# Four block sums per spilled block of a ConvFFN: from GpSimd to VectorE

## Chip, cores and metric

The kernel runs on one core of a Trainium2 chip. The metric is the device time of one execution in microseconds; 2660.22 us is the median of three runs before the change.

## What is computed

The kernel computes a two-layer diffusion trunk over 1024 tokens of 1024 channels. Layer 0 mixes by a long convolution beside differential attention, layer 1 by a chunked gating MLP, and each layer ends with a ConvFFN, the part that the change touches. Cut to that part, the reference is:

```python
D_MODEL, SEQ, D_FF = 1024, 1024, 2816

def dwconv3(u, w, b):
    up = jnp.pad(u, ((0, 0), (1, 1), (0, 0)))
    return up[:, :-2] * w[0] + up[:, 1:-1] * w[1] + up[:, 2:] * w[2] + b

def conv_ffn(h, w_up, conv_w, conv_b, w_down):
    a = dwconv3(h @ w_up, conv_w, conv_b)
    g, u = jnp.split(a, 2, axis=-1)
    return (jax.nn.silu(g) * u) @ w_down
...
for i in range(2):
    ...
    x = x + g1 * mix_x
    x = x + g2 * conv_ffn(modulate(rmsnorm(x, norm_ffn_g[i]), sh2, sc2), ffn_w_up[i], ...)
```

## The kernel before, in words

Every large matrix product of these phases is rewritten in two ways. First, each float32 operand is split into a high part in the fp32r format and a residual, and a product is three matmuls (high x high, high x low, low x high; `mm3`). Second, the operands are cut into 2x2 blocks and multiplied by a Strassen-Winograd scheme with seven products M1 to M7 instead of eight, which needs sums of blocks of each operand beforehand. The seven blocks of the activation side are called B11, B21, B22, T1, T2, T3, T4, and the last four are sums.

A ConvFFN has an up phase and a down phase, and the kernel runs the pair twice, once per layer: the first up phase lies at about 950 to 1420 us, the second at about 1950 to 2420 us. The hidden width 2816 is 22 blocks of 128 rows. An up phase goes through the blocks f = 0, 11, 1, 12, ..., 10, 21, so that two blocks that belong together (k and k + 11) follow each other. For each block f the seven products run in the order M1, M2, M5, M6, M4, M3, M7, with twelve matmuls of 128x128 by 128x512 each, which is 84 a block and 168 a pair; the first three blocks are interleaved. M6 accumulates onto the PSUM bank of M1, M7 onto that of M6, M3 onto that of M5 (`ONTO`, line 1299), so M1's bank must have been copied out before M6 may start. ScalarE does this copy at line 1331, and the others at lines 1337, 1339 and 1341; VectorE adds the rest (lines 1334, 1344, 1347).

The weights of a block are loaded by the SP queue (line 1308), summed by VectorE (`wsums`, line 1288) and split by `hilo_w` (line 1140). Where VectorE is not chosen for the residual, `hilo_w` makes the high part with ScalarE (line 1145), writes its negative with ScalarE (line 1146) and has GpSimd issue a DMA that accumulates the original onto it (line 1147). In the first up phase five of seven products go that way, in the second six of seven (`E_W`, line 56). `hilo` (line 1133) makes the residual with a subtraction on VectorE or GpSimd instead (line 1137).

After M7 of a block, `gated` (line 1589) runs as a background generator, advanced once per step of the main order (`Later.tick`): the convolution as one ScalarE operation (line 1583) and two VectorE operations (lines 1584 and 1586) for each of the two halves, the silu on ScalarE (line 1595), and the product of gate and value on VectorE (line 1597). After every second block it calls `spill` (line 1431), which computes the four sums T1 to T4 of the pair and writes seven blocks to a DRAM tensor Td with four stores. The stores are issued from ScalarE's queue (`st`, line 97). The four sums are the subject of this change. There are 11 spills in an up phase, 22 in all. All additions and subtractions go through the helper of line 132, so profile rows of line 132 hold many uses.

The down phase (`down_steps`, line 1365) reads the blocks back from Td by the SP queue, splits them with `hilo` on GpSimd (line 1472), prepares its weights with sums and residuals on VectorE and GpSimd, and accumulates into the residual stream.

The order of the instructions on each engine is fixed when the kernel is built: a scheduler walks the program in order of priority, where `tc.high_priority(PP)` moves weight preparation and the emptying of banks ahead. At run time each engine takes its instructions strictly in that order, and DMA issues stand in the same queue as the work of the engine that issues them. Tiles named `u` (40 buffers) hold nearly everything in these phases, and `b` is a PSUM bank.

Of the kernel before, what the change touches and what calls it, by code (L numbers as in the profile page):

```python
# [92 lines left out]
def tile_kernel(ctx: ExitStack, tc: tile.TileContext, ap: dict, out: bass.AP, stop=None):  # L93
    nc = tc.nc
    V, A, G, T = nc.vector, nc.scalar, nc.gpsimd, nc.tensor
# [34 lines left out]
    def binop(op):  # L130
        def f(eng, o, a, b):
            eng.tensor_tensor(out=o, in0=a, in1=b, op=op)  # L132
        return f

    add, sub, mul = binop(ADD), binop(SUB), binop(MUL)
# [120 lines left out]
    H0, H1 = slice(0, 512), slice(512, 1024)  # L256
# [870 lines left out]
    def unit(dt=F32):  # L1127
        return up.tile([P, S], dt, tag="u", name=nm("u"))
# [25 lines left out]
    class Later:  # L1154
# [3 lines left out]
        @classmethod  # L1158
        def add(cls, gen, wait=0):
            cls.gens.append([gen, wait])  # L1160
# [270 lines left out]
    def spill(Td, k, b1, b2):  # L1431

        t, s = unit(), unit()
        st(Td[0, :, k], b1[:, H0])
        st(Td[1:3, :, k].rearrange("a p n -> p a n"), b2.rearrange("p (a n) -> p a n", a=2))
        sub(G, s[:, H0], b2[:, H1], b1[:, H1])
        yield 1
        add(G, t[:, H1], s[:, H0], b1[:, H0])
        yield 1
        sub(G, s[:, H1], b2[:, H0], t[:, H1])  # L1440
        st(Td[5:7, :, k].rearrange("a p n -> p a n"), s.rearrange("p (a n) -> p a n", a=2))
        yield 1
        sub(G, t[:, H0], b1[:, H1], b1[:, H0])
        st(Td[3:5, :, k].rearrange("a p n -> p a n"), t.rearrange("p (a n) -> p a n", a=2))

    def in_place(s, m, k, y, z, t3, first="M6"):
# [129 lines left out]
    def ffn(l, after, dst):  # L1576
# [12 lines left out]
        def gated(f, c1, c2):  # L1589
            box = []  # L1590
            yield from conv(c2, NF + f, box)
            yield 1
            yield from conv(c1, f, box)
            u, g = box
            A.activation(g, g, AF.Silu)
            yield 1
            mul(V, g, g, u)
            acts[f] = g
            yield 1
            if f >= nk:  # L1600
                yield from spill(Td, f - nk, acts.pop(f - nk), acts.pop(f))
# [267 lines left out]
```

## Time and profile before

| | us |
|---|---|
| median of three runs | 2660.22 |
| lowest, highest | 2655.24, 2663.31 |
| the profiled execution: its own time | 2657.56 |
| the profiled execution: span from first to last instruction | 2655.8 |
| busy: TensorE matmul / weight load | 2461.9 / 1964.8 |
| busy: VectorE / ScalarE / GpSimd | 1811.5 / 1205.4 / 874.9 |
| granted TensorE clock, mean over the span | 0.972 |

The profile is of one execution. PE is TensorE (PEld its weight loads), DVE is VectorE, ACT is ScalarE, POOL is GpSimd, and a q behind a name is the engine's sequencer, which issues DMAs. A row of a group has line, engine, operation, output and inputs with tile names, the form and the count, then the busy time and the mean of one in ns, and then the idle time of the engine just before such instructions with what ended it. A row of a timeline starts with the start in us and the duration; in square brackets stands how long the engine was idle before it and who released it. "u<-u" alone means that all inputs come from one tile, "u<-u,u" that they come from two. A row of waits has who waited for whom, the total, the number of times and the longest. A granted clock of 1.00 is the full 2.4 GHz.

### The profile page before, as it was taken

How to read it: one execution, taken by the hardware profiler on the slowest of the kernel's cores; microseconds unless marked ns; L12 is line 12 of the kernel's file. 1: busy time of each engine (PE TensorE's matmuls, PEld its weight loads, DVE VectorE, ACT ScalarE, POOL GpSimd, SP SyncE). 2: the span in 40 equal slices, each digit the busy share in tenths (PEclk: the TensorE clock that was granted, in tenths of full speed). 3: DMA queues.
4: the chain of work that ended last, by engine and by line, in shares of the span. 5: the costliest groups of instructions: out<-in, count | busy, mean ns of one | idle time of the engine just before them, and what ended most of it. 6: DMA issues, size and time to landing. Idle time of an engine off the chain costs nothing. (4 is left out here: it accounts for less than half of the span.)

```text
span 2655.8 us, 30417 instructions
## 1 busy us (share of the span) xinstructions
PE 2461.9 (93%) x11192; PEld 1964.8 (74%) x11192; DVE 1811.5 (68%) x2297; ACT 1205.4 (45%) x1875; POOL 874.9 (33%) x649
## 2 busy tenths in 40 slices
PE   6889998798889999999999999999999999999897
PEld 1678987676767776777777787878877777777676
DVE  4888878979995666665656967543467555567844
ACT  2421121137674565655555354323466656564342
POOL 1200112304442013232326574000014343448674
PEclk9999999899999999999999999999999999999998
DMA  7123334277722657888878534012447777778422
GB/s 292 52 103 119 122 105 140 83 222 217 208 69 72 215 136 190 217 229 207 230 193 302 174 120 158 24 47 88 133 90 159 179 176 164 180 175 311 143 74 97
DMA packets 167270, 412.75 MB, mean 155 GB/s; under 512 B 16043, under 2 KB 29359, under 8 KB 164944
## 3 DMA queue, kind: packets, MB, share of 16 engines
q1 hardware_dynamic: 86768, 248.76, 29.3%
q0 software_dynamic: 34848, 63.45, 14.0%
q10 hardware_dynamic: 45504, 98.58, 10.0%
q8 instruction: 88, 1.44, 0.2%
q14 instruction: 62, 0.51, 0.1%
HBM read 261.31 MB, written 85.98 MB: 131 GB/s over the span
## 5 line engine op out<-in xcount | busy, mean ns | idle before, releaser
L154 PE MATMUL b<-u,u 128*128 128x512 f32 (+1 forms) x5624 | 1316.8, 393 | 46.0 <-POOL u L132 19.3
L154 PEld LDWEIGHTS b<-u,u 128*128 128x128 f32 x5624 | 1054.9, 190 | 307.1 <-POOL u L132 26.7
L132 DVE TENSOR_TENSOR u<-u,u 128x512 fp32r<-128x512 f32 (+2 forms) x525 | 470.3, 924 | 314.5 <-ACT u L1136 133.6
L132 POOL TENSOR_TENSOR u<-u,u 128x512 fp32r<-128x512 f32 (+1 forms) x283 | 432.7, 1552 | 189.2 <-ACT u L1136 102.9
L1147 POOL DMA_DIRECT2D u<-u x242 | 211.2, 918 | 560.7 <-ACT u L1146 421.5
L1136 ACT CAST u<-u 128x512 fp32r<-128x512 f32 x462 | 261.4, 616 | 226.7 <-DVE u L132 106.6
L154 PE MATMUL b<-x,u 128*128 128x512 f32 x1224 | 298.5, 399 | 2.7 <-DMA u<-u 2.7
L128 DVE SCALAR_TENSOR_TENSOR u<-u,cols,u 128x1023 f32<-128x1023 f32 x176 | 231.8, 1324 | 95.8 <-ACT u L1583 87.3
L154 PEld LDWEIGHTS b<-x,u 128*128 128x128 f32 x1224 | 230.5, 189 | 64.2 <-DMA u<-u 3.5
L132 POOL TENSOR_TENSOR wlo<-wraw,whi 128x1024 fp32r<-128x1024 f32 x24 | 79.7, 3327 | 401.3 <-ACT whi L147 401.3
L1145 ACT CAST u<-u 128x512 fp32r<-128x512 f32 x242 | 146.3, 615 | 105.5 <-DVE u L132 89.3
L1146 ACT ACTIVATE u<-u 128x512 fp32r<-128x512 f32 x242 | 149.3, 628 | 79.0 <-POOL u L132 70.2
L132 DVE TENSOR_TENSOR u<-u,b 128x512 f32<-128x512 f32 (+1 forms) x132 | 112.4, 861 | 76.6 <-PE b L154 71.1
L132 DVE TENSOR_TENSOR f<-f 128x256 f32<-128x256 f32 (+3 forms) x276 | 152.0, 614 | 0.5 <-DMA Hd<-f 0.2
L1583 ACT ACTIVATE u<-u,cols 128x1024 f32<-128x1024 f32 x88 | 109.2, 1241 | 81.8 <-DVE u L132 81.2
L154 PE MATMUL pj<-hh,whi 128*128 128x512 f32 x320 | 129.1, 405 | 15.6 <-ACT t L736 8.3
L154 PE MATMUL pj<-hl,whi 128*128 128x512 f32 x320 | 128.6, 402 | 3.4 <-DVE hl L132 3.4
L154 PE MATMUL pj<-hh,wlo 128*128 128x512 f32 x320 | 128.2, 401 | 0.0
L128 DVE SCALAR_TENSOR_TENSOR x<-b,mods,x 128x512 f32<-128x512 f32 (+1 forms) x104 | 88.8, 907 | 57.7 <-PE b L154 57.7
L132 POOL TENSOR_TENSOR p<-p,p 128x1280 f32<-128x1280 f32 x27 | 80.1, 2969 | 121.7 <-ACT p L880 103.7
L869 ACT ACTIVATE p<-s,nx 128x1280 f32<-128x1280 f32 x64 | 85.0, 1328 | 45.2 <-DVE nx L865 42.5
L865 DVE TENSOR_REDUCE nx<-s 128x1 f32<-128x1280 f32 x64 | 94.5, 1480 | 4.1 <-PE s L154 3.6
(219 smaller groups left out, 2895.7 us busy)
## 6 DMA issues: line engine op xcount, KB each, us to landing
u<-u POOLq DMA_DIRECT2D x242, 256.0 KB, 4.6
u<-wup SPq DMA_DIRECT2D x88, 512.0 KB, 4.3
Td<-u ACTq DMA_DIRECT2D x66, 512.0 KB, 3.7
u<-Td SPq DMA_DIRECT2D x56, 512.0 KB, 5.1
wraw<-modw SPq DMA_DIRECT2D x48, 512.0 KB, 5.4
u<-wdown SPq DMA_DIRECT2D x40, 512.0 KB, 6.7
wraw<-modw0b SPq DMA_DIRECT2D x32, 512.0 KB, 5.3
xs<-x ACTq DMA_DIRECT2D x48, 256.0 KB, 2.1
```

Of the source, the lines that this page charges most:

```text
L128: eng.scalar_tensor_tensor(out=o, in0=a, scalar=sc, in1=b, op0=op0, op1=op1)
L132: eng.tensor_tensor(out=o, in0=a, in1=b, op=op)
L154: T.matmul(o, l, r, start=st and not onto, stop=sp, skip_group_check=onto)
L865: V.reduce_max(out=q.nx, in_=q.s, axis=AX.X, negate=True)
L869: A.activation(q.p[m], q.s, AF.Exp, bias=q.nx, accum_out=q.l[:, m : m + 1])
L1136: A.copy(out=t[:, H0], in_=x)
L1145: A.copy(out=t[:, H0], in_=x)
L1146: A.activation(t[:, H1], t[:, H0].bitcast(F32), AF.Copy, scale=-1.0)
L1147: G.dma_start(out=t[:, H1], in_=x, accum_op=ADD)
L1583: A.activation(a, c, AF.Identity, bias=col(f"fb{l}", f), scale=col(f"fw{l}1", f))
```

## The change

The four sums of `spill` are issued on VectorE (`V`) in place of GpSimd (`G`). Nothing else in the source differs.

```diff
@@ -1433,14 +1433,14 @@
         t, s = unit(), unit()
         st(Td[0, :, k], b1[:, H0])
         st(Td[1:3, :, k].rearrange("a p n -> p a n"), b2.rearrange("p (a n) -> p a n", a=2))
-        sub(G, s[:, H0], b2[:, H1], b1[:, H1])
+        sub(V, s[:, H0], b2[:, H1], b1[:, H1])
         yield 1
-        add(G, t[:, H1], s[:, H0], b1[:, H0])
+        add(V, t[:, H1], s[:, H0], b1[:, H0])
         yield 1
-        sub(G, s[:, H1], b2[:, H0], t[:, H1])
+        sub(V, s[:, H1], b2[:, H0], t[:, H1])
         st(Td[5:7, :, k].rearrange("a p n -> p a n"), s.rearrange("p (a n) -> p a n", a=2))
         yield 1
-        sub(G, t[:, H0], b1[:, H1], b1[:, H0])
+        sub(V, t[:, H0], b1[:, H1], b1[:, H0])
         st(Td[3:5, :, k].rearrange("a p n -> p a n"), t.rearrange("p (a n) -> p a n", a=2))
```

## Rows read from the trace of the kernel before

**Rows 1.** The page, busy us of each engine, share of the span, instructions

```profile
PE 2461.9 (93%) x11192; PEld 1964.8 (74%) x11192; DVE 1811.5 (68%) x2297; ACT 1205.4 (45%) x1875; POOL 874.9 (33%) x649
```

**Rows 2.** Stretches: length, busy us PE, PEld, DVE, ACT, POOL; clock, DMA share, GB/s

```profile
1050.00:1400.00 350.00, 350.00 (x1619) 268.13 (x1618) 214.48 (x238) 202.31 (x319) 120.24 (x119) 1.00 0.84 219
2000.00:2420.00 420.00, 401.33 (x1713) 324.76 (x1712) 262.48 (x270) 255.12 (x405) 176.41 (x166) 0.98 0.75 186
```

**Rows 3.** Waits from 2000 to 2400 us: who for whom, total, times, longest

```profile
DVE u L132 <- DMA u<-u: 60.6, 23, 4.3
ACT u L1146 <- POOL u L132: 57.8, 10, 6.7
...
PE b L154 <- ACT u L1331: 13.6, 8, 2.9
...
PE b L154 <- DMA u<-u: 5.1, 3, 2.4
```

**Rows 4.** GpSimd's timeline in the second up phase: start, duration, instruction, idle before

```profile
2059.01 2.64 POOL L1147 DMA_DIRECT2D u<-u  x3
...
2216.12 1.68 POOL L132 TENSOR_TENSOR u<-u,u 128x512 f32<-128x512 f32 x1 [8.56 <-DVE u L132]
2217.74 1.75 POOL L1147 DMA_DIRECT2D u<-u  x2
...
2221.38 1.91 POOL L132 TENSOR_TENSOR u<-u,u 128x512 f32<-128x512 f32 x1
```

**Rows 5.** ScalarE's timeline around the same spill

```profile
2216.47 0.63 ACT L1145 CAST u<-u 128x512 fp32r<-128x512 f32 x1 [1.35 <-DVE u L132]
2223.32 0.37 ACTq L1441 DMA_DIRECT2D Td<-u  x1
...
2225.91 0.57 ACT L1331 COPY u<-b 128x512 f32<-128x512 f32 x1
```

**Rows 6.** TensorE's timeline in the second up phase

```profile
2067.17 6.96 PE L154 MATMUL b<-x,u 128*128 128x512 f32 x22 [2.20 <-DMA u<-u]
...
2143.95 7.09 PE L154 MATMUL b<-u,u 128*128 128x512 f32 x24 [2.91 <-ACT u L1331]
...
2226.53 5.73 PE L154 MATMUL b<-u,u 128*128 128x512 f32 x24 [2.91 <-ACT u L1331]
```

**Rows 7.** VectorE's timeline around the same spill, and behind the last one

```profile
2214.21 2.43 DVE L132 TENSOR_TENSOR u<-u,u 128x512 f32<-128x512 f32 x3 [2.30 <-ACT u L1146]
2216.55 1.81 DVE L132 TENSOR_TENSOR u<-u,b 128x512 f32<-128x512 f32 x2
2225.53 2.60 DVE L128 SCALAR_TENSOR_TENSOR u<-u,cols,u 128x1023 f32<-128x1023 f32 x2 [7.16 <-ACT u L1583]
...
2427.24 0.85 DVE L132 TENSOR_TENSOR u<-u,u 128x512 fp32r<-128x512 f32 x1 [5.80 <-ACT u L1136]
```

**Rows 8.** Groups of instructions by line, engine and shape, whole span

```profile
L132 POOL TENSOR_TENSOR u<-u,u 128x512 f32<-128x512 f32 x66 | 105.8, 1603 | 82.1 <-DVE u L132 67.9 <-issue 12.2 <-PE b L154 1.0
...
L132 POOL TENSOR_TENSOR u<-u 128x512 f32<-128x512 f32 x22 | 39.1, 1778 | 0.0
...
L132 DVE TENSOR_TENSOR u<-u,u 128x512 fp32r<-128x512 f32 x245 | 223.3, 930 | 135.2 <-ACT u L1136 133.6 <-POOL u L132 1.2
...
L132 DVE TENSOR_TENSOR u<-u 128x512 f32<-128x512 f32 x44 | 30.2, 685 | 0.2
```

**Rows 9.** Stretches, columns as in rows 2

```profile
2143.95:2150.88 6.93, 6.92 (x24) 5.65 (x25) 4.70 (x5) 5.81 (x9) 2.58 (x3) 0.79 1.03 210
...
2226.53:2232.11 5.58, 5.58 (x25) 4.61 (x26) 4.71 (x5) 5.04 (x8) 2.58 (x3) 1.00 0.95 213
...
2442.00:2505.00 63.00, 53.83 (x217) 42.15 (x215) 61.18 (x60) 18.24 (x33) 41.11 (x26) 0.95 0.41 137
```

**Rows 10.** Waits from 1400 to 1460 us, then from 2400 to 2435 us

```profile
PE b L154 <- POOL u L132: 2.1, 2, 1.7
...
PE b L154 <- POOL u L132: 2.4, 2, 1.7
```

## The prediction

> **What bounds the kernel now.** I read the page first, then the busy time of every engine by stretch, then the waits of the two up phases, and last the timeline of one pair of blocks, engine by engine. The page shows TensorE busy for 93% of the span and GpSimd for 33% [rows 1], which says little about a stage. By stretch the two up phases, which run the same code on two layers, differ [rows 2]. Between 1050 and 1400 us TensorE is busy for all of 350 us at clock 1.00. Between 2000 and 2420 us it is busy for 401.3 of 420 at 0.98. So only the second phase has holes in it, some 19 us.
>
> The waits name them [rows 3]: TensorE waits 13.6 us in 8 places for the ScalarE copy of line 1331 (it empties M1's bank, and M6 accumulates onto that bank) and 5.1 us in 3 places for the accumulating DMAs that finish the weights. One step back, ScalarE waits 57.8 us in 10 places for a GpSimd operation of line 132. There are ten spills in that stretch.
>
> One pair shows the chain. GpSimd takes the first of the four sums at 2216.12, then two DMA issues that stand ahead in its queue, then the other three, and ends at 2223.29 [rows 4]. ScalarE's queue holds the store of line 1441, which needs the last of these, and everything behind it stands still from 2217.1 until 2223.32; the copy of line 1331 starts at 2225.91 and ends at 2226.48 [rows 5]. TensorE restarts at 2226.53 after an idle 2.91 us [rows 6]. VectorE itself is idle for 7.16 us there, because its next input comes from the blocked ScalarE [rows 7]. The hold costs TensorE up to 2.91 us a pair, and a hold some 3.3 us long (6.2 less 2.9) would cost nothing.
>
> **The change part by part.** *Removed:* 22 spills x 4 = 88 sums on GpSimd, 66 of mean 1603 ns and 22 of mean 1778 ns [rows 8]: 105.8 + 39.1 = 144.9 us of GpSimd, which is no term by itself. What counts is their place in two in-order queues.
>
> *Added:* 88 sums on VectorE. The nearest row is a sum of the same form, 128x512 float32 with both inputs in SBUF, at a mean of 685 ns [rows 8]. The upper bound is the same subtraction with an fp32r output, much of it in stretches where GpSimd computes too: 930 ns [rows 8]. I take 0.69, since GpSimd has only DMA issues left there: 88 x 0.685 = 60.3 us, 40 of them (27.4 us) between 2000 and 2420 us. The cover is VectorE's idle time: 420 - 262.5 = 157.5 us [rows 2]. If that cover were gone, 2.7 to 3.7 us a pair would delay the weight sums that share the queue.
>
> *Waits:* the sums read what VectorE itself has just written, so the wait from VectorE to GpSimd goes and no input wait replaces it. Their two fresh buffers might not be free yet; on GpSimd no row shows a wait for that worth naming, so I take nothing and bound it by one weight load's delay, 4 us once or twice. No DMA is added or removed. The four stores stay in ScalarE's queue; two of them now wait for VectorE where they waited for GpSimd. SP's queue issues none of the moved work.
>
> *Where the end of the fourth sum goes:* it comes 7.2 us after the first can start today. On VectorE it comes after 4 x 0.69 = 2.7 us, or 4.6 us if the two bank sums of 1.81 us are taken in between [rows 7]. ScalarE is released 2.6 to 4.4 us sooner. The two longest holes are 2.91 us, so **the 13.6 us fall to nothing or to about 0.6 in all; I take -12**, and the bounds are 0 and -13.6.
>
> *The accumulating DMAs:* GpSimd issues them in order, so its sums push them back. Before the hole that ends at 2067.17 three of them leave only from 2059.01 on, back to back behind a spill's sums [rows 4, 6]; none of the three holes of this kind lies far from a spill. The bounds are 0 and -5.1; that row is nearest to the full size, and I take -4.5.
>
> *The clock:* after some holes the granted clock falls. In the stretch from 2143.95, before which TensorE had been idle for 2.91 us, it reads 0.79, a mixture of the levels of 2.4 and 1.2 GHz, and 24 matmuls take 6.92 us. In the stretch from 2226.53 it reads 1.00 after an equal hole, all at the level of 2.4 GHz, and as many take 5.58 us, 0.2325 each [rows 6, 9]. The difference is 1.34 us. Four holes of the second phase are followed by such a stretch: 4 x 1.34 = 5.4 us. The bounds are 0 and -8.4 (0.02 of 420 us [rows 2]); I take the -5.4.
>
> *The ends of the two up phases:* the last sums stand on GpSimd ahead of the residual parts (line 1137) that the first down products need. TensorE waits 2.1 us for them after the first phase and 2.4 after the second [rows 10]: 4.5 us. The second time VectorE is idle for 5.80 us there [rows 7], which covers the 2.7 that it gets. I take -4, with bounds 0 and -4.5. Behind this lies a stretch in which VectorE is the limit (61.2 of 63 us busy [rows 9]). It may gain what VectorE does earlier, or lose what it does more: -3 to +2.7 each time, nearest to 0 because the four sums come before it. I take 0.
>
> *The first up phase:* TensorE has no hole, so 0; bounds 0 and +3, one late weight.
>
> The sum is -12 - 4.5 - 5.4 - 4 = -26. Once TensorE is no longer held, something else is late next: the phase runs one more accumulating DMA a block than the first one, and its pair must shrink from 41.3 us (2143.95 to 2226.53 is two of them [rows 6]) to 39.1 (168 matmuls at 0.2325). For that I give back 5 us, half a microsecond a pair. That leaves -21 from the profiled execution, which took 2657.56 us (its span 2655.8 and 1.8 around it). It lies 2.7 us under the median of the three runs, 2660.22. So 2657.6 - 21 = 2636.6, and **I forecast 2637 us**. With every term at its far bound and nothing given back (-13.6 - 5.1 - 8.4 - 4.5 - 6) it would be 2620; I put the lower end at 2624, since they hardly come all together. With half of the sum it would be 2647. A measurement of this kernel tells about 0.3% from no change, that is 8 us.
>
> **The rivals.** *No change, since TensorE is the limit.* The holes close and open again elsewhere, because weights, DMA or the bank sums are only a little earlier than TensorE. For it: TensorE is at 95% of that phase already [rows 2], and the DMA engines are busy for 0.75 of it. Against it: the first phase runs the same steps with 0.84 of DMA and no hole. With 0 to 8 us left of the sum it would give 2650 to 2658, say 2655. The Trainium skill (Perfetto Trace Analysis, Identifying the Most-Contended Engine) tells one to work first on the engine with the highest occupancy; read by the whole span that is TensorE, and relieving GpSimd at 33% would return nothing, 2657.6. By that rule the trace agrees only in the first up phase; in the second the holes of rows 3 disagree.
>
> *Slower: VectorE holds ScalarE longer than GpSimd did.* The order of each queue is settled at build time. If the fourth sum is placed behind the next weight sums, which wait for an accumulating DMA (60.6 us in 23 waits, longest 4.3 [rows 3]), ScalarE stands at the store through that wait and two or three weight sums, 4.3 + 3 x 0.69 = 6.4 us longer. It decides from a hold of 3.3 us on, and beyond that every microsecond is TensorE's: ten pairs at 6.4 more than today come to 64 us in the second phase, and if half of the pairs are hit, 32, so 2690. For it: the product of gate and value already sits behind such a wait at 2214.21 [rows 7]. Against it: the sums follow that product directly in program order, and VectorE's next wait is one for ScalarE.
>
> *The change does not do what it says:* four engine names are swapped, and that cannot fail. But all queues are ordered anew, and a few microseconds of either sign can come from it; that is inside the range.
>
> **How the numbers follow.** The forecast has 0.75, almost all of it beyond 8 us; no change 0.15; slower 0.08; 0.02 for a queue order that gives or takes a few microseconds. Of the forecast some 0.03 lies within 8 us. So faster 0.74, same 0.18, slower 0.08. The forecast's own range is 2624 to 2650; to leave out no more than 0.2 the range goes on through the case of no change, to 2658.
>
> **What would show it.** In the changed profile GpSimd has no float32 sum of 128x512 left in the up phases and VectorE has 88 more near 0.69 us. ScalarE's 57.8 us of waiting for GpSimd are gone, with a wait for VectorE of some 2 to 4 us a spill in their place. TensorE's 13.6 and 5.1 us fall below 5 together, the clock of the second phase reads 0.99 or more, and a pair takes 39 to 40 us. I am wrong if ScalarE's hold is as long as before with VectorE as its releaser, if TensorE's holes have only changed their releaser, or if the first phase shows holes of its own.

## The result, and the profile after

The changed kernel takes **2637.11 us** (median of four runs, 2627.86 to 2640.53), the kernel before beside it 2661.53 (four runs). The ratio is 0.9898 [0.9877, 0.9918]: 24.4 us less, and 2637 was forecast. The profiled execution took 2627.86 us, the shortest of its four, with a span of 2625.7. Against the 2655.8 of the profiled execution before that is 30.1 less, of which 4.1 us lie ahead of the first changed instruction, in code that is the same. A single profiled execution is good to about 5 us: in the stretch between the two ConvFFNs, which no kernel here touches, the profiled executions took 344.5 to 350.8 us.

First the page of the changed kernel, engine by engine, which answers to [rows 1]:

```profile
PE 2446.5 (93%) x11192; PEld 1958.3 (75%) x11192; DVE 1855.1 (71%) x2385; ACT 1208.6 (46%) x1875; POOL 759.9 (29%) x561
```

The 88 instructions have moved: 2297 became 2385 on VectorE, 649 became 561 on GpSimd. VectorE's groups by form over the whole span, the second of which answers to the last of [rows 8]:

```profile
L132 DVE TENSOR_TENSOR u<-u,u 128x512 f32<-128x512 f32 x302 | 241.1, 815 | 165.1 <-DMA u<-u 93.6 <-ACT u L1741 48.7 <-issue 9.6
...
L132 DVE TENSOR_TENSOR u<-u 128x512 f32<-128x512 f32 x66 | 47.3, 717 | 0.2
```

To compare the two kernels where the order of the work is the same, I cut the second up phase at its first and its last convolution. The convolution's line 1583 in the trace before, then after (count, duration min/median/max, first and last start):

```profile
L1583 ACT ACTIVATE u<-u,cols x44: 1227/1242/1250, 2004.8 to 2404.8; 128x1024 f32<-128x1024 f32 x44
```

```profile
L1583 ACT ACTIVATE u<-u,cols x44: 1227/1243/1248, 1998.9 to 2378.0; 128x1024 f32<-128x1024 f32 x44
```

The phase went from 400.0 to 379.1 us. The busy time by stretch over exactly this phase, before and then after (columns as in rows 2), with the two stretches of [rows 2] in the second fence:

```profile
2004.80:2404.80 400.00, 381.33 (x1625) 308.33 (x1623) 244.48 (x258) 245.98 (x392) 162.29 (x158) 0.98 0.75 179
```

```profile
1050.00:1400.00 350.00, 349.83 (x1618) 266.91 (x1617) 226.88 (x272) 200.41 (x316) 70.72 (x81) 1.00 0.83 217
1998.90:2378.00 379.10, 373.25 (x1620) 304.86 (x1619) 264.87 (x298) 248.64 (x391) 104.90 (x118) 1.00 0.79 190
2000.00:2420.00 420.00, 413.86 (x1798) 338.13 (x1797) 301.87 (x324) 268.62 (x426) 143.07 (x142) 1.00 0.81 206
```

Read the second number: TensorE's idle time fell from 400.0 - 381.3 = 18.7 to 379.1 - 373.3 = 5.8 us, that is 12.8 less, and its busy time by 8.1 us for nearly the same number of recorded matmuls, since the granted clock went from 0.98 to 1.00. Together they are the 20.9 us. Between 1050 and 1400 us the first up phase had no hole, and it has 0.17 us of one now.

Waits from 2000 to 2400 us, which answer to [rows 3]:

```profile
DVE u L132 <- DMA u<-u: 55.4, 22, 4.9
ACT u L1145 <- DVE u L132: 54.8, 18, 8.2
ACT u L1583 <- DVE u L132: 39.7, 16, 5.8
...
PE b L154 <- DMA u<-u: 5.7, 2, 3.5
...
PEld b L154 <- ACT u L1331: 0.2, 1, 0.2
```

ScalarE no longer waits for GpSimd's operations; it waits for VectorE. TensorE waits for the copy of line 1331 in no place at all. ScalarE around one spill, to be read beside [rows 5]:

```profile
2195.95 0.37 ACTq L1435 DMA_DIRECT2D Td<-u  x1
...
2199.20 0.37 ACTq L1441 DMA_DIRECT2D Td<-u  x1
2199.60 1.16 ACTq L1444 DMA_DIRECT2D Td<-u  x1
2201.76 1.24 ACT L1583 ACTIVATE u<-u,cols 128x1024 f32<-128x1024 f32 x1 [3.18 <-DVE u L132]
...
2203.42 0.58 ACT L1331 COPY u<-b 128x512 f32<-128x512 f32 x1
```

ScalarE still stands idle for 3.18 us around the two stores, and TensorE doesn't feel it. The store of line 1441 leaves at 2199.20; what ends the idle time is VectorE's bank sum for M7, which the convolution reads:

```profile
2200.50 1.22 DVE L132 TENSOR_TENSOR u<-u,b 128x1024 f32<-128x1024 f32 x1 [0.74 <-issue]
```

TensorE's timeline, beside [rows 6]:

```profile
2046.88 8.06 PE L154 MATMUL b<-u,u 128*128 128x512 f32 x34 [2.19 <-DMA u<-u]
...
2058.87 6.97 PE L154 MATMUL b<-x,u 128*128 128x512 f32 x22 [3.46 <-DMA u<-u]
...
2156.18 5.78 PE L154 MATMUL b<-x,u 128*128 128x512 f32 x24
...
2194.63 5.55 PE L154 MATMUL b<-x,u 128*128 128x512 f32 x23
```

Two holes are left, both at the start of the phase and both for late weights. From 2156.18 to 2194.63 one pair takes 38.45 us, 168 matmuls at 0.229, without a hole; before, the five pairs from 2143.95 on took 40.4 to 41.9.

### The profile page after: what moved, and what is told of

Its sections match the earlier page's. It is cut to its first block, busy times and chain, and to the rows that moved or that the text cites. A ratio compares the mean times of both kernels' runs of the same rounds, so it can differ in the third digit from the quotient of the medians.

```text
span 2625.7 us, 30408 instructions
## 1 busy us (share of the span) xinstructions
PE 2446.5 (93%) x11192; PEld 1958.3 (75%) x11192; DVE 1855.1 (71%) x2385; ACT 1208.6 (46%) x1875; POOL 759.9 (29%) x561
## 4 chain that ended last, share of the span: by engine, by line
PE 37%; issue 14%; DVE 8%; POOL 5%; DMA 3%; ACT 2%; POOLq 0%; ACTq 0%; SPq 0%; DVEq 0%
PE b L154 35%; DVE u L132 5%; POOL u L132 4%; PE s L154 2%; ACT u L1136 1%; DMA u<-u 1%; DVE x L128 1%; DVE u L128 1%; DVE x L132 1%; POOL u L1147 1%; DMA u<-wdown 0%; DMA u<-Td 0%; DMA Td<-u 0%; DVE u L1221 0%; DMA wraw<-modw 0%
## 5 line engine op out<-in xcount | busy, mean ns | idle before, releaser
L132 DVE TENSOR_TENSOR u<-u,u 128x512 f32<-128x512 f32 (+2 forms) x591 | 500.5, 875 | 276.3 <-ACT u L1136 100.0
L132 POOL TENSOR_TENSOR u<-u,u 128x512 fp32r<-128x512 f32 x217 | 332.5, 1564 | 113.4 <-ACT u L1136 109.3
```

## The experiments

The question was what the sums on GpSimd had cost. Three candidates: the **hold** (ScalarE stands at the store of line 1441, and the copy of line 1331 behind it comes late), the **queue** (the sums stand ahead of GpSimd's accumulating DMAs), and the **reading** (GpSimd's sums and VectorE's operations on two SBUF tiles slow each other). The first two are the prediction's, the third it left at nothing. All kernels at a glance; the phase is the second up phase from first to last convolution of the profiled execution, and the two columns behind it are TensorE's waits in it, all in us.

| kernel | median | ratio to before, 95% | phase | for L1331 | for DMA |
|---|---|---|---|---|---|
| before | 2661.53 | | 400.0 | 13.6 | 5.1 |
| changed | 2637.11 | 0.9898 [0.9877, 0.9918] | 379.1 | 0 | 5.7 |
| 1 changed, second phase only | 2643.07 | 0.9925 [0.9904, 0.9946] | 377.7 | 0 | 5.0 |
| 2 changed + unread sums on GpSimd | 2692.38 | 1.0109 [1.0086, 1.0132] | 414.2 | 18.8 | 5.0 |
| 3 changed + fills on GpSimd | 2643.51 | 0.9919 [0.9888, 0.995] | 379.3 | 0.7 | 3.7 |
| 4 changed + sums doubled on VectorE | 2646.36 | 0.9943 [0.9925, 0.9961] | 388.2 | 9.1 | 1.4 |
| 5 as 4, stores by SP | 2653.29 | 0.9956 [0.9939, 0.9974] | 381.1 | 4.6 | 1.8 |
| 6 before, stores by SP | 2661.1 | 0.9994 [0.9978, 1.001] | 399.0 | 1.0 | 15.9 |
| 7 before, stores by GpSimd | 2670.17 | 1.003 [1.0015, 1.0045] | 385.9 | 1.4 | 7.8 |
| 8 changed, stores by GpSimd | 2651.86 | 0.9955 [0.994, 0.9971] | 376.2 | 0.5 | 2.5 |
| 9 before, ten of eleven stores by GpSimd | 2651.51 | 0.996 [0.9946, 0.9974] | 387.7 | 1.3 | 9.8 |
| 10 fills, and a hold by 8 columns | 2641.27 | 0.9922 [0.9895, 0.9949] | 382.6 | 0 | 8.7 |
| 11 fills, and a hold by a copy | 2650.02 | 0.9951 [0.9933, 0.9969] | 384.4 | 0.8 | 5.7 |
| 12 changed, VectorE residual for M1's weights | 2633.51 | 0.9888 [0.986, 0.9916] | 380.5 | 0 | 3.0 |

### 1. Where: the second phase alone

```diff
-    def spill(Td, k, b1, b2):
+    def spill(Td, k, b1, b2, e):
...
-        sub(V, s[:, H0], b2[:, H1], b1[:, H1])
+        sub(e, s[:, H0], b2[:, H1], b1[:, H1])
...
-                yield from spill(Td, f - nk, acts.pop(f - nk), acts.pop(f))
+                yield from spill(Td, f - nk, acts.pop(f - nk), acts.pop(f), V if l else G)
```

> The sums on VectorE in the second up phase alone, on GpSimd in the first as before. Both theories of the hold place the gain in the second phase, where TensorE had holes: 20 to 23 us of the 24, the rest being what the end of the first phase gained (2 to 3 us). If the first phase mattered more than its holes say, less than 16 us stay.

Measured: 2643.07 us, 0.75% less than before where the full change gives 1.02%. Against the kernel before beside it (2662.43) that is 19.4 us, just under the 20 to 23 expected. About three quarters of the gain come with the eleven spills of the second phase, though the two intervals overlap. The second up phase has the same sums here as in the changed kernel, and took 377.7 us against 379.1: so well does this number repeat. The first down phase, behind an up phase left as it was, took 178.9 us in the profiled execution (last convolution to the next norm's statistics), in the changed kernel 173.2; that is hardly more than one execution can tell.

### 2. The reading: the same sums on GpSimd, read by nobody

The changed kernel, with the four sums repeated on GpSimd into a scratch tile. Nothing waits for them.

```diff
+        z = sp.tile([P, 512], F32, tag="sq", name=nm("sq"), bufs=4)
         sub(V, s[:, H0], b2[:, H1], b1[:, H1])
+        sub(G, z, b2[:, H1], b1[:, H1])
...
         add(V, t[:, H1], s[:, H0], b1[:, H0])
+        add(G, z, z, b1[:, H0])
...
         sub(V, s[:, H1], b2[:, H0], t[:, H1])
+        sub(G, z, b2[:, H0], z)
...
         sub(V, t[:, H0], b1[:, H1], b1[:, H0])
+        sub(G, z, b1[:, H1], b1[:, H0])
```

> The changed kernel, with the four sums done a second time on GpSimd from the same blocks into a scratch tile that nobody reads. So GpSimd's queue is as full as before (88 sums of 1.3 to 1.9 us ahead of its DMA issues, beside VectorE), but no store and no ScalarE instruction waits for them. Theory 1 (ScalarE's queue is held by the two stores that wait for GpSimd): most of the gain stays, 20 us or more of the 24 against the kernel before, and TensorE's waits for the copy of line 1331 stay near 0. Theory 2 (GpSimd's sums push the accumulating DMAs back, or slow VectorE beside them): the gain falls to 10 us or less, and TensorE waits for accumulating DMAs, 10 us or more in the second up phase.

Measured: 2692.38 us, 55 more than the changed kernel and 30 more than the kernel before beside it (2662.43). VectorE's groups in the second up phase, in the changed kernel and then in this one:

```profile
L132 DVE TENSOR_TENSOR u<-u,u 128x512 f32<-128x512 f32 x84 | 57.8, 689 | 68.5 <-DMA u<-u 55.4 <-issue 9.6 <-ACT u L1146 1.8
...
L132 DVE TENSOR_TENSOR u<-u 128x512 f32<-128x512 f32 x28 | 19.1, 683 | 0.0
L132 DVE TENSOR_TENSOR u<-u,u 128x512 fp32r<-128x512 f32 x21 | 16.2, 772 | 5.2 <-ACT u L1136 5.2
```

```profile
L132 DVE TENSOR_TENSOR u<-u,u 128x512 f32<-128x512 f32 x84 | 78.4, 934 | 66.6 <-DMA u<-u 54.0 <-issue 6.6 <-ACT u L1145 3.1
L132 DVE TENSOR_TENSOR u<-u 128x512 f32<-128x512 f32 x28 | 39.4, 1408 | 0.0
...
L132 DVE TENSOR_TENSOR u<-u,b 128x512 f32<-128x512 f32 x38 | 25.8, 679 | 2.4 <-PE b L154 2.4
...
L132 DVE TENSOR_TENSOR u<-u,u 128x512 fp32r<-128x512 f32 x21 | 24.9, 1185 | 4.0 <-ACT u L1136 4.0
```

The same instructions take 934, 1408 and 1185 ns instead of 689, 683 and 772. Those that take one input from PSUM (u<-u,b) stay at 679. The convolutions of line 128 read two SBUF tiles too and stay at 1282 ns; at the spill of 2157 us they start at 2168.65, when GpSimd's sums have ended at 2165.06. Everything that VectorE has in its queue shifts, the sums that the stores wait for and the bank sum that the convolution reads, and ScalarE with them: TensorE's waits for the copy of line 1331 are back at 18.8 us. The gain is lost as theory 2 had it, but not through the accumulating DMAs, for which TensorE waits 5.0 us where 10 or more were expected. The unread sums also keep the blocks' buffers longer; the weights did not come later for that, since VectorE waits 54.0 us for DMAs here and 55.4 in the changed kernel. So sums on GpSimd cost time that no wait for GpSimd shows. The Trainium skill (SBUF — State Buffer, Who interferes with whom) says that a VectorE instruction with two SBUF inputs contends with a GpSimd instruction that reads SBUF; this trace agrees on who is slowed.

### 3. The queue: GpSimd busy as long, without reading

```diff
+        z = sp.tile([P, 512], F32, tag="sq", name=nm("sq"), bufs=4)
+        add(V, z[:, 0:4], b2[:, 0:4], b1[:, 0:4])
+        for _ in range(10):
+            G.memset(z, 0.0)
```

> The changed kernel, with ten memsets of 128x512 on GpSimd per spill, released by a tiny VectorE operation at the place of the first sum, into a scratch tile that nobody reads. GpSimd's queue is as full as with the four sums (some 5 us a spill ahead of its DMA issues), but it reads nothing from SBUF and nobody waits for it. Theory 2a (the sums push the accumulating DMAs back in GpSimd's queue): the time returns towards the kernel before, 2655 to 2665 us, with TensorE waiting 10 us or more for accumulating DMAs. Theory 2b (GpSimd's sums slow VectorE's operations beside them, each by their reads): no sum slows VectorE here, and the time stays at the changed kernel's, 2632 to 2645 us; the loss of the idle sums then came from the slower VectorE.

Measured: 2643.51 us, 6 more than the changed kernel. GpSimd's groups in the second up phase:

```profile
L1147 POOL DMA_DIRECT2D u<-u x112 | 97.2, 928 | 151.5 <-ACT u L1146 141.7 <-DVE u L132 5.7 <-ACT u L1599 2.3
L1437 POOL MEMSET sq<- 128x512 f32 x100 | 62.1, 621 | 72.0 <-DVE sq L132 67.8
```

6.2 us of fills a spill stand in GpSimd's queue between the accumulating DMAs, about as long as the four sums did (4 x 1.6), and the phase takes 379.3 us where the changed kernel took 379.1. VectorE's groups keep their durations (690 and 773 ns). Run 2 adds about as much on GpSimd (69 us in the phase) and reads SBUF; what differs is the reading, and that VectorE's three groups of run 2 take 50 us more. This tests the queue in one order, with the DMAs among the fills: **fills that stand ahead of the accumulating DMAs cost nothing in the phase**. Run 9 below has an order in which work ahead of them does cost. The 6 us of the median lie elsewhere: in the profiled execution the two down phases took 178.7 and 167.1 us against 173.2 and 164.4 in the changed kernel, and the untouched stretch between the ConvFFNs 349.9 against 345.4. What makes these longer I have not traced.

### 4 and 5. ScalarE made late by VectorE

Run 4 doubles the four sums on VectorE into a scratch tile, so that the last two stores come three and four sums, 2.1 and 2.7 us, later, without GpSimd. Run 5 gives these two stores to the SP queue.

```diff
+        z = sp.tile([P, 512], F32, tag="sq", name=nm("sq"), bufs=4)
+        sub(V, z, b2[:, H1], b1[:, H1])
         sub(V, s[:, H0], b2[:, H1], b1[:, H1])
...
-        st(Td[5:7, :, k].rearrange("a p n -> p a n"), s.rearrange("p (a n) -> p a n", a=2))
+        ld(Td[5:7, :, k].rearrange("a p n -> p a n"), s.rearrange("p (a n) -> p a n", a=2))
```

(the first two lines and their three likes in both, the last two and the store of line 1444 in run 5 alone)

> The changed kernel with every one of the four sums done twice on VectorE, the second time into a scratch tile that nobody reads: 88 more operations of 0.69 us, 60 us of VectorE work. If VectorE's idle time covers the sums (the prediction's cost of nothing), the time is within 5 us of the changed kernel. If each sum on VectorE already costs something on the path, the doubled ones cost the same again or more: 10 us and up, and then the change alone has hidden a cost of that size.

> The sums doubled on VectorE, which brought back 9.1 us of TensorE waiting for the copy of line 1331, with the two last stores issued from SP's queue, so that ScalarE cannot be held by them. If the doubled sums cost through the hold: these 9.1 us fall below 2. Whether the time follows depends on what the stores do to the weight loads behind them in SP's queue: 2637 us if nothing, up to 2655 if they delay them as in the run with the stores moved alone (TensorE waited 15.9 us for accumulating DMAs there).

Measured: run 4 2646.36 us, 9 more than the changed kernel, and the phase 388.2, 9.1 us of which TensorE waits for line 1331. That lies between the two cases expected, within 5 us and from 10 us up. One spill of run 4, ScalarE, then VectorE's bank sum for M7, then TensorE (its source lines are shifted by five, the convolution is L1588):

```profile
2180.47 0.37 ACTq L1445 DMA_DIRECT2D Td<-u  x1
2182.28 0.37 ACTq L1449 DMA_DIRECT2D Td<-u  x1
2183.41 1.25 ACT L1588 ACTIVATE u<-u,cols 128x1024 f32<-128x1024 f32 x1 [5.58 <-DVE u L132]
...
2185.06 0.57 ACT L1331 COPY u<-b 128x512 f32<-128x512 f32 x1
```

```profile
2182.16 1.21 DVE L132 TENSOR_TENSOR u<-u,b 128x1024 f32<-128x1024 f32 x1
```

```profile
2185.69 5.73 PE L154 MATMUL b<-u,u 128*128 128x512 f32 x24 [0.94 <-ACT u L1331]
```

ScalarE idle for 5.58 us costs TensorE 0.94; in the changed kernel 3.18 cost it nothing. Both stores have left by 2182.65, and the convolution starts at 2183.41, as soon as the bank sum has ended: this sum stands in VectorE's queue behind the doubled sums, and the copy of line 1331 stands in ScalarE's queue behind the convolution. So run 4 does not make the hold at a store by itself. In run 5 the waits for line 1331 halve to 4.6, where less than 2 was expected, and the phase is back at 381.1. One spill of run 5, where neither of the two last stores is in ScalarE's queue:

```profile
2107.49 1.24 ACT L1588 ACTIVATE u<-u,cols 128x1024 f32<-128x1024 f32 x1 [4.64 <-DVE u L132]
```

```profile
2109.77 5.73 PE L154 MATMUL b<-u,u 128*128 128x512 f32 x24 [2.23 <-ACT u L1331]
```

Here too the bank sum ends last, at 2107.45. So TensorE pays when ScalarE comes late to line 1331, whatever made it late, and about half of what run 4 pays remains with the stores out of the way. How much it pays does not follow from the idle time alone: 4.64 us cost 2.23 here, and 2.61 at another spill of run 4. Run 5 as a whole is slower again, 2653.29: its two down phases took 183.7 and 170.0 us against 173.2 and 164.4 in the changed kernel. There TensorE waits for GpSimd and VectorE (9.4 and 5.6 us after the first up phase, 5.5 and 0.4 in the changed kernel); how the stores' queue leads to that I have not traced.

### 6. The hold taken away: stores by SP

The kernel before, sums on GpSimd, with the two stores that wait for them issued by SP.

```diff
-        st(Td[5:7, :, k].rearrange("a p n -> p a n"), s.rearrange("p (a n) -> p a n", a=2))
+        ld(Td[5:7, :, k].rearrange("a p n -> p a n"), s.rearrange("p (a n) -> p a n", a=2))
...
-        st(Td[3:5, :, k].rearrange("a p n -> p a n"), t.rearrange("p (a n) -> p a n", a=2))
+        ld(Td[3:5, :, k].rearrange("a p n -> p a n"), t.rearrange("p (a n) -> p a n", a=2))
```

> The kernel before, sums on GpSimd, with only the two stores that wait for the sums moved from ScalarE's queue to SP's. Theory 1: ScalarE is no longer held, its 57.8 us of waiting for GpSimd in the second up phase fall below 10, TensorE's 13.6 us for the copy of line 1331 below 3, and the kernel gains 14 to 22 us without any sum on VectorE (what the two ends of the up phases gained, some 3 us each, may stay away, and the weight loads behind the stores in SP's queue may cost a few). Theory 2: GpSimd is as full as before, so the gain is below 6 us.

Measured: 2661.1 us, no gain. The waits for line 1331 fell from 13.6 to 1.0 us and those for weights rose from 5.1 to 15.9, in 22 places. Waits of the SP queue in the second up phase:

```profile
SPq L1441 <- POOL u L132: 130.3, 10, 17.5
SPq L1308 <- DVE u L128: 93.9, 7, 19.8
```

This run misleads if only its time is read: SP, which loads the weights, now stands at the store for 130.3 us in ten spills. It moves the hold from one queue to another, and tells nothing on what removing it is worth.

### 7 to 9. The hold taken away for good: stores by GpSimd

GpSimd issues the two stores behind its own sums, so that no other queue waits for them. Run 7 does it in the kernel before, run 8 in the changed kernel as a control. Run 9 is run 7 without the eleventh spill, the one at the boundary.

```diff
-        st(Td[5:7, :, k].rearrange("a p n -> p a n"), s.rearrange("p (a n) -> p a n", a=2))
+        G.dma_start(out=Td[5:7, :, k].rearrange("a p n -> p a n"), in_=s.rearrange("p (a n) -> p a n", a=2))
...
+        (G.dma_start if k < 10 else st)(Td[5:7, :, k].rearrange("a p n -> p a n"), s.rearrange("p (a n) -> p a n", a=2))
```

(the last line in run 9; the store of line 1444 likewise)

> The kernel before (sums on GpSimd), with the two last stores of each spill issued by GpSimd itself, right behind its sums: nothing in ScalarE's queue or in SP's waits for GpSimd's sums any more, and no weight load stands behind a store. Theory 1 (the hold of ScalarE at the stores is the cost of the sums on GpSimd): TensorE's waits for the copy of line 1331 fall below 3 us and most of the gain of the change is there, 2640 to 2647. Theory 2 (the sums on GpSimd make the weights late by themselves: they stand ahead of the accumulating DMAs and slow VectorE's operations beside them): TensorE waits for accumulating DMAs instead, 12 us or more in 2000 to 2400, and the time stays at 2653 to 2664.

> The changed kernel (sums on VectorE) with the same two stores issued by GpSimd: the control of the run before, since the two DMA issues now stand in GpSimd's queue ahead of accumulating DMAs, and GpSimd waits there for VectorE's sums. Both theories: 2632 to 2642, as the changed kernel, if that costs little; by 5 us or more above it, 2642 to 2650, if the issues and their wait are what makes weights late, and then the run before has to be read less that cost.

> The kernel before (sums on GpSimd), with the two last stores of a spill issued by GpSimd for the first ten spills of each up phase; the eleventh, at the boundary to the down phase, stays as before. Theory 1 (the hold of ScalarE is more than half of what the sums on GpSimd cost, and the run with all eleven spills lost its gain at the boundaries): the second up phase, from its first to its last convolution, takes 386 us as there (before 400.0, after 379.1), the down phases 176 and 167 as before, and the time falls to 2645 to 2652. Theory 2 (the hold is worth little by itself): the up phase goes back to 395 or more, and the time is 2656 to 2666.

Measured: run 7 2670.17, run 8 2651.86, run 9 2651.51 us. Run 7's time lies above both ranges, and its phase speaks for theory 1: it takes 385.9 us, 14.1 less than before, with 1.4 us of waits for line 1331 and 7.8 for DMAs where theory 2 had 12 or more, while the two down phases grew from 175.8 and 167.1 to 185.9 and 172.9. Run 9 was made to part the two, and went as theory 1 had it in time and phase: 0.4% faster than before, 387.7 us (the first down phase, 179.9 in this execution, did not come back to 176). **Without the hold in ten of eleven spills, 10.6 us of the 27 are there that the full change gives by the ratios (0.40% and 1.02%), and 12.3 of 20.9 us in the phase.** This is what the hold was worth less what the two stores cost in GpSimd's queue.

Where the other 8.6 us of the phase are shows TensorE's timeline in run 9:

```profile
2051.37 7.52 PE L154 MATMUL b<-u,u 128*128 128x512 f32 x22 [4.87 <-DMA u<-u]
...
2110.94 8.01 PE L154 MATMUL b<-u,u 128*128 128x512 f32 x34 [0.79 <-DMA u<-u]
...
2391.20 3.08 PE L154 MATMUL b<-x,u 128*128 128x512 f32 x12 [1.91 <-DMA u<-u]
2396.18 3.53 PE L154 MATMUL b<-x,u 128*128 128x512 f32 x10 [1.90 <-DMA u<-u]
```

Between 2119 and 2391 us there is no hole, with GpSimd still computing the sums: in the steady pairs the hold was all that they cost. What is left sits at the start of the phase and at its end, as late weights. At the start they are late in GpSimd's queue (run 9):

```profile
2038.70 3.64 POOL L132 TENSOR_TENSOR u<-u,u 128x512 f32<-128x512 f32 x2 [1.77 <-DVE u L132]
...
2048.30 3.89 POOL L1147 DMA_DIRECT2D u<-u  x4
```

From 2038.70 to 2052.19 GpSimd has no gap: the four sums, the two stores and five accumulating DMAs follow each other. The first of these DMAs leaves at 2046.99, though ScalarE had written its input by 2041.42 (line 1146), and the hole that ends at 2051.37 is a wait for such a DMA. Run 8, with the same stores and without the sums, waits 2.5 us for DMAs in the whole phase. So the queue costs here, which the order of run 3 did not bring out. VectorE has grown slower too, as one spill and run 9's groups of the phase show:

```profile
2225.24 4.32 DVE L128 SCALAR_TENSOR_TENSOR u<-u,cols,u 128x1023 f32<-128x1023 f32 x2 [1.31 <-ACT u L1583]
```

```profile
L128 DVE SCALAR_TENSOR_TENSOR u<-u,cols,u 128x1023 f32<-128x1023 f32 x85 | 124.9, 1477 | 24.9 <-ACT u L1583 23.6
...
L132 DVE TENSOR_TENSOR u<-u,u 128x512 fp32r<-128x512 f32 x21 | 25.4, 1210 | 14.8 <-ACT u L1136 12.1 <-issue 2.7
```

In the changed kernel these take 1281 and 772 ns. In the kernel before, the first took 1297: VectorE stood idle beside the sums because its input came from the held ScalarE [rows 7]. With the hold gone the convolution runs beside the sums: at 2225.24 two of its operations take 4.32 us, while GpSimd's sums go on to 2227.15, and the two at 2230.08 take 2.60. So 85 x 0.18 = 15 us of VectorE time come in. In the steady pairs VectorE's idle time takes them up; whether they make the weights late at the two ends, beside the queue, is not shown. The same step from the other side is run 7 against run 8, where only the engine of the sums differs and neither holds ScalarE: 18.3 us in the medians, 9.7 in the phase, the queue and the reading together.

Run 8 lies above both ranges expected of it, and not because of the up phase, which is the shortest of all at 376.2. At the start of the second down phase TensorE has one hole of 19.66 us. TensorE there, then GpSimd, then VectorE (run 8):

```profile
2422.70 53.80 PE L154 MATMUL b<-u,u 128*128 128x512 f32 x227 [19.66 <-DVE u L132]
```

```profile
2400.47 2.56 POOL L132 TENSOR_TENSOR u<-u,u 128x512 fp32r<-128x512 f32 x2
2402.96 0.75 POOL L1441 DMA_DIRECT2D Td<-u  x1
2403.74 18.36 POOL L132 TENSOR_TENSOR u<-u,u 128x512 fp32r<-128x512 f32 x15
```

```profile
2400.20 22.45 DVE L132 TENSOR_TENSOR u<-u,u 128x512 fp32r<-128x512 f32 x1
```

One VectorE subtraction of 128x512 is in progress for 22.45 us, some thirty times its usual 0.77, while GpSimd takes 17 subtractions on SBUF tiles, with one DMA issue of 0.75 us among them, and it ends 0.55 us after GpSimd's row. That these subtractions are what keeps it is likely and not shown.

### 10 and 11. A hold made with fills: two that made none

Both add to run 3. In run 10 the last 8 columns of the third sum are computed by GpSimd behind the fills, in run 11 a ScalarE copy of 8 columns of the filled tile stands ahead of the store.

```diff
-        sub(V, s[:, H1], b2[:, H0], t[:, H1])
+        sub(V, s[:, 512:1016], b2[:, 0:504], t[:, 512:1016])
+        sub(G, s[:, 1016:], b2[:, 504:512], t[:, 1016:])
...
+        A.copy(out=z[:, 0:8], in_=z[:, 8:16])
```

> The kernel with the memsets, with the last 8 columns of the third sum done by GpSimd behind them, so that one of the stores in ScalarE's queue waits for GpSimd's queue as before. Theory 1 (the hold of ScalarE is what costs): slower than the kernel with the memsets by 10 to 20 us in the second up phase, TensorE waits 8 us or more for the copy of line 1331 there. If the hold does not matter by itself: within 5 us of it.

> The changed kernel with ten GpSimd fills of an unread tile per spill (some 0.62 us each, no reading of SBUF) and, in ScalarE's queue ahead of the store of line 1441, a copy of 8 columns of that tile, which has to wait for the last fill: ScalarE is held for some 5 us a spill without any GpSimd sum. Theory 1: TensorE's waits for the copy of line 1331 return, 8 us or more in 2000 to 2400, and the time goes back to 2650 to 2662. Theory 2: the hold by itself costs less than half of the 24 us, 2640 to 2649.

Measured: 2641.27 and 2650.02 us. Neither is a test of the hold. In run 10 the small subtraction was placed after the second fill instead of the last, and ScalarE waited for GpSimd in two places for 2.0 us in all. In run 11 it waited, in the second up phase, for

```profile
ACT sq L1445 <- POOL sq L1437: 10.2, 10, 4.6
```

1.0 us a spill where some 5 were meant, and TensorE waited 0.8 us for line 1331 where theory 1 expected 8 or more. That its median reached 2650 is therefore not theory 1's doing, though the number is at the edge of what it expected; what costs these 13 us stays open.

### 12. One more set of weights on VectorE

The two holes that are left come from late weights, so the second up phase gets the first one's choice: the residual of one more product on VectorE instead of an accumulating DMA.

```diff
-E_W, E_D, E_O = ("VGGVGGG", "VGGVGGG", "GGGVGGG"), ...
+E_W, E_D, E_O = ("VGGVGGG", "VGGVGGG", "VGGVGGG"), ...
```

> The changed kernel with M1's weights in the second up phase split by VectorE, as in the first phase, so that five of seven products go through the accumulating DMA and not six. The changed kernel's remaining holes of the second up phase are 5.7 us of waiting for accumulating DMAs and one stretch of lower clock behind them. If one DMA less a block removes them: 4 to 8 us faster than the changed kernel, 2629 to 2633 us. If these holes come from late weight loads at the start of the phase: no change, 2634 to 2640 us. 22 subtractions more on VectorE may take some of it back.

Measured: 2633.51 us, 0.9888 [0.986, 0.9916], between the two ranges expected; the interval covers the changed kernel's 0.9898. TensorE's waits for weights fell from 5.7 to 3.0, and the phase did not become shorter, 380.5. No version here beats the changed kernel by more than can be measured.

## Why the prediction was right

The time was right to 0.1 us of the median, and that it came so near is luck: the forecast took 21 us off one profiled execution of 2657.6, while the median of the kernel before is 2661.53 beside the change, and the medians lie 24.4 apart. From execution to execution the sum was -21; measured are 30.1 less the 4.1 ahead of the change, -26. By its steps:

- **The hold and its chain were right.** -12 was taken and all 13.6 us of waits for line 1331 went. ScalarE's idle time at the spill shown is 3.18 us, inside the forecast 2 to 4, and costs TensorE nothing. The break-even of 3.3 us is not confirmed by that, since the idle time ends there with the bank sum and not with the stores, and in runs 4 and 5 its length alone does not tell what TensorE pays. Run 9 shows the hold removed; no run makes it by itself.
- **The clock** was put at -5.4 with -8.4 as its bound; TensorE's busy time in the phase fell by 8.1, at 1.00 where it was 0.98 (five more matmuls recorded before are 1.2 of it). The mechanism was right, the size nearer to the bound.
- **The accumulating DMAs were wrong.** -4.5 was taken because GpSimd's sums push the DMAs back [rows 4], and these waits went from 5.1 to 5.7 us. The step that failed is "none of the three holes of this kind lies far from a spill": one of them is [rows 6]'s 2.20 us at 2067.17, at the start of the phase, and in the changed kernel the holes are still there, 2.19 and 3.46 us. The mechanism itself is there: run 3 shows no cost of other work ahead of these DMAs, but run 9 has a hole of 4.87 us behind them.
- **The give-back of 5 us was wrong too**, and by the same size the other way: a pair takes 38.45 us, less than the 39.1 for which something late was expected. These two errors cancel (+0.5 forecast, +0.6 measured). The second up phase was put at -12 - 4.5 - 5.4 + 5 = -16.9 and gave -20.9.
- **The ends of the phases** were put at -4. The waits of 2.1 and 2.4 us [rows 10] became 0 and 0.3, and the two down phases took 2.6 and 2.7 us less, 5.3 together. One execution each hardly carries these differences: run 1's first down phase, behind an up phase as before, took 178.9 us where the kernel before took 175.8.
- **VectorE's cost** was right at 0. Its busy time in the phase rose by 20.4 us (244.5 to 264.9), while 40 sums at 0.69 are 27.4: its own subtractions became 3.1 us cheaper beside a GpSimd that no longer sums (21 x (918 - 772) ns), its convolutions 1.4 us.
- **What the prediction left out is the reading.** It took 0.685 us a sum and noted that the fp32r subtraction ran at 930 ns "much of it in stretches where GpSimd computes too" [rows 8], yet gave no term to sums that slow VectorE. In the kernel before little of this showed, since the hold kept VectorE idle beside the sums. Run 2 shows what it can cost, and run 8 perhaps an extreme of it. Run 9 shows that the prediction's main cause buys 10.6 us with the sums still on GpSimd; the rest needs the sums off GpSimd, and lies at the starts and ends of the phases. How it divides between the reading and GpSimd's queue, no run tells.

Of the rivals, no change through an engine that is the limit did not come, and the rule of the Trainium skill (Perfetto Trace Analysis, Identifying the Most-Contended Engine) holds in the first of the two up phases alone: there TensorE was busy for 350.00 of 350 us before the change, and the phase went from 422.7 to 423.2 us. The slower rival, a VectorE that holds ScalarE longer, did not come either; run 4 comes nearest to it, though there the bank sum is late and not the store.

## What to carry to other kernels

Work on a side engine can cost more than its busy share tells, by the queue that waits for its result, by what stands behind it in its own queue, and by the engine that it slows where both read SBUF; look for all three, and remember that the first can hide the others. Remove a suspected wait without handing it to another queue, and read the stage as well as the total: run 7 lost at the boundaries what it gained in the phase, and run 6 only moved the wait.

## What the runs showed of the hardware

- VectorE operations with two SBUF inputs slow down beside GpSimd's sums by a factor of 1.4 to 2.1 on the mean of a group (run 2), while those with one input from PSUM keep their 0.68 us, and beside fills on GpSimd they keep theirs (690 and 773 ns, run 3). The convolutions, with two SBUF inputs too, keep 1282 ns in run 2, where they come after the sums, and take 1477 in run 9, where they run beside them.
- Beside GpSimd subtractions that follow each other closely, a single VectorE subtraction lasted 22.45 us (run 8). The Trainium skill (SBUF — State Buffer, SBUF: two separate sides) says that whichever of the two starts first has the shared port pair for its whole instruction, and the other blocks. By the starts of the rows this trace does not agree: the VectorE row begins 0.27 us before GpSimd's and still ends after 17 of GpSimd's. Why, no run here tells.
